# SwiGLU of a two-layer step on one core: plain 128-row tiles against Strassen's seven products over two of three token chunks

## The chip, the cores and the metric

The kernel runs on one core of a Trainium2 chip. The metric is the device time of one execution, in microseconds (us). Before the change the median of three runs is 3021.92 us, from 3016.77 to 3026.52.

## What is computed

A two-layer encoder step: layer 0 mixes tokens with forgetting attention, layer 1 with sliding-window attention, and both end with the same tail, the part that is changed:

```python
h = h + _rms(mix, norm_mix_post[i])
f = _swiglu(_rms(h, norm_ffn_pre[i]), ffn_w_gate[i], ffn_w_up[i], ffn_w_down[i])
h = h + _rms(f, norm_ffn_post[i])
gate = jax.nn.sigmoid(_rms(h, ple_norm[i]) @ ple_w_gate[i] + ple_b_gate[i])
h = h + gate * (p[i] @ ple_w_proj[i])
# _swiglu(a, g, u, d) = (silu(a @ g) * (a @ u)) @ d
# _rms(x, g) = x * rsqrt(mean(x * x) + EPS) * g
```

`mix` is the attention output times `w_out`. The model width is 1024 (`KT`=8 blocks of 128), the hidden width 2816 (`FFT`=22 blocks). The 1024 prompt tokens and 128 sample tokens make 1152 columns, in three chunks of `C`=384 (`NC3`=3). All is float32.

## The kernel before

Activations stand feature-major: a chunk is a tile of 128 partitions by 8 blocks by 384 tokens. A float32 product is made of three fast ones. Each operand is split into a rounded high part (`round_r`, L133, a cast on ACT) and the remainder (`low_part`, L139, a subtraction on DVE), and `mm3` (L229 to L231) issues weight-high times activation-high, weight-high times activation-low and weight-low times activation-high into one PSUM bank:

```python
nc.tensor.matmul(ps, w[0], a[0], start=first, stop=False)
nc.tensor.matmul(ps, w[0], a[1], start=False, stop=False)
nc.tensor.matmul(ps, w[1], a[0], start=False, stop=last)
```

A hidden tile (128 hidden features of one chunk) takes 24 such matmuls of 128x384 for gate and 24 for up (`feat`). `gu` makes both, and `act_hidden` makes Silu on ACT (L1216), times up on DVE (L1218), and the split on both. `down_tile` multiplies two hidden blocks with `w_down` into a fresh bank (6 matmuls per output block), and `down_out` adds the bank to `y` on DVE (L1252). Group g is two hidden blocks of all three chunks, so 288 gate/up matmuls and then 144 of down; a tail has 11 groups. The hidden tiles never leave SBUF.

Ahead of the groups, `serpentine` walks `w_out` over the three chunks. After a chunk's last tile come an RMS root (`plan_rms`: squares on ACT, sums on DVE L379/L381, `pstat` on PE, Newton steps on DVE L255 to L261, `prms` on PE, copy `rr` on ACT L394), the residual (`plan_residual`: a scale L469 and an add L473 for each block, the old row loaded through `st`, three buffers), a second root, and the normed and split operand (`plan_normed`, L419). After the groups comes the same with `y`, then the gate projection and, in layer 0, the projections of layer 1.

Two things order the work. `Plan` is a list scheduler that runs when the kernel is built: each step has an engine, an assumed cost, predecessors, buffers that it takes and frees, and a due time; `run` places the steps, and each engine then executes its queue in the order so found. Before, a plan covers `w_out` with group 0, and another the last group with the gates; groups 1 to 9 stand in program order, with the high-priority marks of `gu` and `down_out`. SP issues nearly all DMAs, in its own order. `act` is a pool of nine 12 KB slots (operands, `y`), `wraw`, `whi` and `wlo` hold weight units of 128x1024.

In time: projections and layer 0's attention until about 617 us, tail 0 until about 1700 (with `w_out` to about 720), layer 1's attention until about 1960, tail 1 to the end.

Of the kernel before, what the change touches and what calls it, by code (L numbers as in the profile page):

```python
# [37 lines left out]
OSP=3  # L38
SST=(1,6)
NPC=8  # L40
# [44 lines left out]
def tile_kernel(ctx: ExitStack, tc: tile.TileContext, i, o, upto=99):  # L85
# [32 lines left out]
    q2s_d = dr.tile([D, P], F32, name="q2s_d")  # L118

# [83 lines left out]
    def presplit(specs, dst):  # L203

        for u, (src, gain) in enumerate(specs):
            for q in range(4):
                cs = slice(q * 256, (q + 1) * 256)
                raw = tp.tile([P, C], F32, name="st", tag="st", bufs=STB)[:, :256]
                nc.sync.dma_start(raw, src[:, cs])
                yield  # L210
                keep = tc.keep_in_program_order
                if gain is not None:
                    nk = gain[2] // 4
                    k0 = gain[1] + q * nk
                    r3 = raw.rearrange("p (k c) -> p k c", k=nk)
                    g = gains[:, gain[0], k0:k0 + nk].unsqueeze(2).to_broadcast([P, nk, 256 // nk])
                    keep(nc.vector.tensor_tensor(r3, r3, g, MULT))
                hl = tp.tile([P, 2, C], F32R, name="sq", tag="sq", bufs=2)[:, :, :256]
                keep(nc.scalar.copy(hl[:, 0], raw))
                keep(nc.vector.tensor_tensor(hl[:, 1], raw, hl[:, 0].bitcast(F32), SUB))  # L220
                nc.sync.dma_start(dst[u][:, :, cs], hl.bitcast(F32))
                yield

# [3 lines left out]
    def mm3(ps, w, a, first, last):  # L227

        nc.tensor.matmul(ps, w[0], a[0], start=first, stop=False)  # L229
        nc.tensor.matmul(ps, w[0], a[1], start=False, stop=False)  # L230
        nc.tensor.matmul(ps, w[1], a[0], start=False, stop=last)  # L231
# [39 lines left out]
    class Plan:  # L271
# [19 lines left out]
        def run(self):  # L291
# [23 lines left out]
            while left:  # L315
# [16 lines left out]
                for u in users[n]:  # L332
                    early[u] = max(early[u], end + (LAG[engine] if engine != LOAD or steps[u][0] != LOAD else 0.0))
# [30 lines left out]
    def plan_rms(plan, src, after, out="rr", slot=None, ready=()):  # L364
# [4 lines left out]
        def square(k):  # L369
            if k:  # L370
                box[k] = t = tp.tile([P, 2, C], F32, name="sq", tag="sq", bufs=2)
# [20 lines left out]
        def copy():  # L392
            box["r"] = r = slot() if slot else tp.tile([P, C], F32, name="rr", tag=out, bufs=2)
            nc.scalar.copy(r, box["pr"][:, :C])  # L394
# [10 lines left out]

    def plan_normed(plan, src, rms, g, put, free=()):


        (r, box), out, tmp, first = rms, [], {}, []

        def scale(k):
            if not out:
                out.extend((act_slot(F32R, "ahi"), act_slot(F32R, "alo")))
                put(tuple(out))
            tmp[k] = t = tp.tile([P, C], F32, name="tmp", tag="tmp", bufs=2)
            if g is None:
                nc.vector.tensor_tensor(t, src()[:, k, :], box["r"], MULT)
            else:
                nc.vector.scalar_tensor_tensor(t, src()[:, k, :], gains[:, g, k:k + 1], box["r"], MULT, MULT)  # L419

        def high(k):
            round_r("a", out[0][:, k, :], tmp[k])

        def low(k):
            low_part(out[1][:, k, :], tmp.pop(k), out[0][:, k, :])

        done = []
        for k in range(KT):
            x = plan.add(DVE, 0.53, step(scale, k), [r] + first, takes=["tmp"] + ([] if first else ["act", "act"]))
            first = first or [x]  # L430
            x = plan.add(ACT, 0.42, step(high, k), [x])

            done.append(plan.add(DVE, 0.47, step(low, k), [x] + done[-1:],
                                 frees=["tmp"] + (["rr", *free] if k == KT - 1 else [])))
        return done
# [23 lines left out]
    def plan_residual(plan, y, rms, g, hsrc, c, then=lambda k: None):  # L459
# [16 lines left out]
        done, loads = [], []  # L476
        for k in range(KT):
            loads = [plan.add(LOAD, 0.55, step(load, k), loads, takes=["hs"])]
# [36 lines left out]
    def out_parts(ks):  # L515
# [3 lines left out]
        def split(k):  # L519
            if not parts:  # L520
                parts.extend((act_slot(F32R, "ohi"), act_slot(F32R, "olo")))
            keep(round_r("a", parts[0][:, k, :], oc[0][:, k, :]))
            keep(low_part(parts[1][:, k, :], oc[0][:, k, :], parts[0][:, k, :]))
# [548 lines left out]
    for hp in range(8):  # L1072
        pair, g = nxt, 0
        for m in ORDER:
# [8 lines left out]
            if hp == 7 and m == ORDER[0]:  # L1083
                oa0, beside = out_parts(range(KT - 1))
# [26 lines left out]
    def layer_tail(l, oc, Wo, oa0, specs_kv=(), more=None, more_rms=None):  # L1111
# [7 lines left out]
        oa, mix, a, y, b = ([None] * NC3 for _ in range(5))  # L1119
        tiles, hid = {}, {}  # L1120

        def put(where, c):
            return functools.partial(where.__setitem__, c)

        def tile_steps(key, unit, act, needs_w, needs_a, frees=(), pieces=2):
# [7 lines left out]
            for p in range(pieces):  # L1133
                x = plan.tile(3.92 / pieces, step(piece, p * n, n), [x] + needs_a[p * n:(p + 1) * n], takes=["mm"] if p == 0 else [],
# [3 lines left out]
        def serpentine(plan, W, at, act, needs, then, free):  # L1138
# [788 lines left out]
```

## Time and profile before

| quantity | value |
|---|---|
| median of three runs | 3021.92 us |
| profiled execution, its own time | 3016.32 us |
| its span in the profile | 3014.3 us |
| PE busy | 2981.8 us of the span |
| DVE, ACT, POOL busy | 1568.5, 1006.6, 197.7 us |
| DMA | 362.34 MB, mean 120 GB/s |
| granted TensorE clock | 0.999 of full speed |

PE is TensorE, PEld its weight loads, which run beside the matmuls; DVE is VectorE, ACT ScalarE, POOL GpSimd, SP the engine that issues DMAs. `L229` is line 229 of the kernel; `pgu<-ahi,whi` names the output tile and its inputs. Matmuls are pipelined, so the time that one costs in a stream is the distance between two starts, not its duration. `[2.12 <-DVE acc]` behind a row says that the engine idled 2.12 us before it, until DVE wrote `acc`.

### The profile page before, as it was taken

The numbers are of one execution on the slowest core, as the hardware profiler recorded it, in microseconds if no ns is written. First come the engines' busy times: TensorE is split into PE (matmuls) and PEld (weight loads), VectorE is DVE, ScalarE is ACT, GpSimd is POOL, SyncE is SP. The second block draws the span as 40 slices with busy tenths as digits, with TensorE's granted clock in tenths as the row PEclk, the third lists the DMA queues.
The fourth block names the chain that finished last, engine by engine and source line by source line (L and its number), as shares of the span: only waits on it lengthen the run. The fifth ranks groups of instructions, "written<-read, shape, count | busy, mean of one in ns | idle before, by whom it ended". The sixth has DMA issues, their size and how long they took to land. (4 is left out here: it accounts for less than half of the span.)

```text
span 3014.3 us, 47129 instructions
## 1 busy us (share of the span) xinstructions
PE 2981.8 (99%) x18356; PEld 2870.2 (95%) x18356; DVE 1568.5 (52%) x3657; ACT 1006.6 (33%) x2150; POOL 197.7 (7%) x324
## 2 busy tenths in 40 slices
PE   8999999999999999999999999999999999999999
PEld 8999877799999999999999998799999999999999
DVE  6253477758444444444389446658333333333486
ACT  6221367645322222221144255744311111111142
POOL 0000245400000000000000022300000000000000
PEclk9999999999999999999999999999999999999999
DMA  7364577433122222222156567434111111111064
GB/s 255 106 203 143 165 197 199 116 120 131 67 95 95 95 95 95 95 95 87 35 181 197 201 209 218 125 121 137 62 64 63 64 63 63 64 63 61 15 201 148
DMA packets 236178, 362.34 MB, mean 120 GB/s; under 512 B 32130, under 2 KB 189188, under 8 KB 235924
## 3 DMA queue, kind: packets, MB, share of 16 engines
q1 hardware_dynamic: 235956, 359.34, 37.4%
q8 instruction: 144, 2.36, 0.3%
q14 instruction: 78, 0.64, 0.1%
HBM read 263.82 MB, written 97.27 MB: 120 GB/s over the span
## 5 line engine op out<-in xcount | busy, mean ns | idle before, releaser
L229 PE MATMUL pgu<-ahi,whi 128*128 128x384 f32 x1728 | 577.4, 334 | 0.0
L230 PE MATMUL pgu<-alo,whi 128*128 128x384 f32 x1728 | 577.4, 334 | 0.0
L231 PE MATMUL pgu<-ahi,wlo 128*128 128x384 f32 x1728 | 577.3, 334 | 0.0
L229 PE MATMUL ps<-ahi,whi 128*128 128x384 f32 x1392 | 471.3, 339 | 1.0 <-ACT ev L634 0.7
L231 PE MATMUL ps<-ahi,wlo 128*128 128x384 f32 x1392 | 466.7, 335 | 1.2 <-DMA wlo<-wkq_d 1.2
L230 PE MATMUL ps<-alo,whi 128*128 128x384 f32 x1392 | 466.2, 335 | 0.0
L230 PE MATMUL pd<-hlo,whi 128*128 128x384 f32 x1056 | 357.8, 339 | 2.8 <-DVE hlo L139 2.6
L229 PE MATMUL pd<-hhi,whi 128*128 128x384 f32 x1056 | 358.0, 339 | 0.8 <-ACT hhi L133 0.8
L231 PE MATMUL pd<-hhi,wlo 128*128 128x384 f32 x1056 | 357.2, 338 | 0.0
L1252 DVE TENSOR_TENSOR y<-y,pd 128x384 f32<-128x384 f32 x480 | 262.0, 552 | 175.1 <-PE pd L231 174.7
L133 ACT CAST whi<-wraw 128x1024 fp32r<-128x1024 f32 (+3 forms) x190 | 192.9, 1024 | 472.7 <-PE pd L230 216.9
L139 DVE TENSOR_TENSOR wlo<-wraw,whi 128x1024 fp32r<-128x1024 f32 (+3 forms) x190 | 225.4, 1189 | 211.7 <-ACT whi L133 211.4
L230 PEld LDWEIGHTS pgu<-alo,whi 128*128 128x128 f32 x1728 | 324.5, 188 | 0.0
L231 PEld LDWEIGHTS pgu<-ahi,wlo 128*128 128x128 f32 x1728 | 324.5, 188 | 0.0
L229 PEld LDWEIGHTS pgu<-ahi,whi 128*128 128x128 f32 x1728 | 324.5, 188 | 0.0
L1218 DVE TENSOR_TENSOR sil<-sil,pgu 128x384 f32<-128x384 f32 x108 | 59.8, 554 | 462.1 <-PE pgu L231 462.1
L229 PEld LDWEIGHTS ps<-ahi,whi 128*128 128x128 f32 x1392 | 262.0, 188 | 7.0 <-issue 4.9
L231 PEld LDWEIGHTS ps<-ahi,wlo 128*128 128x128 f32 x1392 | 261.7, 188 | 2.2 <-DMA wlo<-wkq_d 2.2
L230 PEld LDWEIGHTS ps<-alo,whi 128*128 128x128 f32 x1392 | 262.1, 188 | 0.0
L230 PEld LDWEIGHTS pd<-hlo,whi 128*128 128x128 f32 x1056 | 198.3, 188 | 4.4 <-DVE hlo L139 4.4
L229 PEld LDWEIGHTS pd<-hhi,whi 128*128 128x128 f32 x1056 | 198.3, 188 | 1.7 <-ACT hhi L133 1.7
L231 PEld LDWEIGHTS pd<-hhi,wlo 128*128 128x128 f32 x1056 | 198.3, 188 | 0.0
(223 smaller groups left out, 4311.6 us busy)
## 6 DMA issues: line engine op xcount, KB each, us to landing
wraw<-in_w_gate SPq DMA_DIRECT2D x44, 512.0 KB
wraw<-in_w_up SPq DMA_DIRECT2D x44, 512.0 KB
wraw<-in_w_down SPq DMA_DIRECT2D x44, 512.0 KB
wpg_d<-sq SPq DMA_DIRECT2D x64, 256.0 KB
st<-h_d SPq DMA_DIRECT2D x72, 192.0 KB
wraw<-in_w_out SPq DMA_DIRECT2D x24, 512.0 KB
wkq_d<-sq SPq DMA_DIRECT2D x48, 256.0 KB
whi<-wpg_d SPq DMA_DIRECT2D x24, 512.0 KB
```

Of the source, the lines that this page charges most:

```text
L133: return nc.scalar.copy(out, in_)
L139: return nc.vector.tensor_tensor(out, x, hi.bitcast(F32), SUB)
L229: nc.tensor.matmul(ps, w[0], a[0], start=first, stop=False)
L230: nc.tensor.matmul(ps, w[0], a[1], start=False, stop=False)
L231: nc.tensor.matmul(ps, w[1], a[0], start=False, stop=last)
L1218: nc.vector.tensor_tensor(tiles[key], tiles[key], tiles.pop((key, 1))[:, :C], MULT)
L1252: nc.vector.tensor_tensor(y[c][:, f, :], y[c][:, f, :], ps[:, :C], ADD)
```

## The change

Gate, up and down are computed by the Strassen-Winograd scheme for two chunks together, cA and cB (`TAILS`: 1 and 2 in layer 0, 2 and 1 in layer 1). The third, cC = 0, stays plain.

For gate and up, a group is one weight pair (two blocks of 128 hidden features) by two halves of the model width, against two chunks by the same two halves. Instead of eight block products of 12 matmuls there are seven (`product`): operands `Y11`, `Y21`, `Y22` are halves of the normed chunks, `T1` to `T4` are sums and differences of them (`minus`, made once a tail in place, then split by `operand`), and of the weights two units are raw (A, B) and two are made of sums of halves (C, D; `s_sum`, four DVE additions of 128x512 for each matrix). The sums are held in the two `wide` buffers (tag `y`) that hold the mixed chunks cA and cB until their operands are made. Products add up in banks X, Y and Z, and X is copied out between products. The plain tiles of cC (`ps<-chi`) stand between the products, but for the first two matrices (`EARLY`), whose four plain tiles run ahead of all products.

The hidden rows then go to DRAM: 22 plain ones (`hc_d`) and 7 combinations for each of 11 pairs (`t_d`). Down is done last, as 44 ksteps for cC and 77 for the two chunks in each tail. `kstep` loads one 192 KB row back, splits it, splits half a unit of `w_down` (kept in the `act` slots as it came, changed in place between passes) and issues 12 matmuls into four banks, which are read only at the end of a pass. Each kstep takes two of the ten `row` slots (`NROW`). The additions L1252 are gone.

One `Plan` now covers a whole tail, `presplit` (the preparation of later weights) included. After down the chunks come in the order cC, cB, cA.

```diff
+NROW=10
+TAILS=((0, 1, 2), (0, 2, 1))
...
+    t_d = dr.tile([7, FFT // 2, P, C], F32, name="t_d")
+    hc_d = dr.tile([FFT, P, C], F32, name="hc_d")
...
+        operand("Y11", cA, 0)
+        operand("Y21", cA, 4)
+        operand("Y22", cB, 4)
+        minus(cA, 0, (cB, 0), (cA, 0))
+        operand("T1", cA, 0)
+        minus(cB, 0, (cB, 4), (cB, 0))
+        operand("T3", cB, 0)
+        minus(cB, 4, (cB, 4), (cA, 0))
+        operand("T2", cB, 4)
+        minus(cA, 4, (cA, 4), (cB, 4))
+        operand("T4", cA, 4)
...
+                args = {1: (s[:, 0, X1], x2()[:, X1], x2()[:, X2], ADD), 2: (s[:, 0, X2], s[:, 0, X1], x1()[:, X1], SUB),
+                        3: (s[:, 1, X1], x1()[:, X1], x2()[:, X1], SUB), 4: (s[:, 1, X2], x1()[:, X2], s[:, 0, X2], SUB)}
+                nc.vector.tensor_tensor(*args[n])
...
+                    if new:
+                        tiles[m, bank] = psmm.tile([P, 512], F32, name="p" + bank, tag="mm")
+                    a_ = acts[name]
+                    hi, lo = units_[m, u]
+                    for j in range(4):
+                        ws = slice(half * 512 + j * P, half * 512 + (j + 1) * P)
+                        mm3(tiles[m, bank][:, :C], (hi[:, ws], lo[:, ws]), (a_[:, j], a_[:, 4 + j]), new and j == 0, j == 3, more=not new)
...
+            product("X", "A", 0, "Y11", new=True)
+            copied("11", "X")
+            if not early:
+                plain(0, "A", [])
+                plain_out(0)
+            product("Z", "A", 1, "Y21", new=True, frees=[wa])
+            added("11", "Z", ["mm"])
+            product("X", "C", 1, "T2")
+            product("Y", "D", 0, "T3", new=True)
+            product("X", "C", 0, "T1", frees=[wc])
...
+            if not early:
+                plain(1, "B", [])
+                plain_out(1)
+            product("X", "D", 1, "Y22", frees=[wd])
+            product("Y", "B", 1, "T4", frees=[wb])
...
+                diff("u11", "r12", "r11")
+                store("r11", t_d[0, g], ("t", 0, g))
+                diff("r12", "r22", "r12")
+                diff("u22", "r22", "u11")
...
+        EARLY = (0, 0), (0, 1)
+        for m in EARLY:
+            matrix(*m, when=0)
         for g in range(FFT // 2):
-            for f in (2 * g, 2 * g + 1):
-                specs += [(i["w_gate"][l, f], None), (i["w_up"][l, f], None)]
...
+            def h_load():
+                hp[s] = [None, row(F32R)]
+                nc.sync.dma_start(hp[s][1].bitcast(F32), hsrc)
...
+            x = add(LOAD, 0.85, h_load, r=[hkey], after=last_row, takes=["row", "row"])
+            last_row[:] = [x]
+            x = add(ACT, 0.42, h_high, after=[x])
+            h_done = add(DVE, 0.47, h_low, after=[x])
+            x = add(ACT, 0.51, w_high, r=[wkey], after=plan.turn.get(f"w{t}", []), takes=[f"w{t}"])
+            plan.turn[f"w{t}"] = [x]
+            w_done = add(DVE, 0.6, w_low, r=[wkey], after=[x])
...
+                for d in ds:
+                    if new and start:
+                        tiles["D", d] = psmm.tile([P, 512], F32, name="pd", tag="mm")
+                    ds_ = slice(d * P, (d + 1) * P)
+                    mm3(tiles["D", d][:, :C], (parts_[s][0][:, ds_], parts_[s][1][:, ds_]), hp[s], new and start, stop, more=not new)
...
-        def gu(g, fi, c):
-            wg, wu = W.get(6 * g + 2 * fi), W.get(6 * g + 2 * fi + 1)
-            key = g, fi, c
-            for n, w in enumerate((wg, wu)):
-                tiles[key, n] = psmm.tile([P, 512], F32, name="pgu", tag="mm")
-                feat(tiles[key, n][:, :C], w, a[c])
...
-        def down_tile(g, c, f, fis=(0, 1)):
-            if 0 in fis:
-                tiles[c, f] = psmm.tile([P, 512], F32, name="pd", tag="mm")
-            fs = slice(f * P, (f + 1) * P)
-            for fi in fis:
-                wd = W.get(6 * g + 4 + fi)
-                mm3(tiles[c, f][:, :C], (wd[0][:, fs], wd[1][:, fs]), hid[g, fi, c], fi == 0, fi == 1)
...
-        def group_steps(g, order, loaded, needs, last_c, free):
...
-        for g in range(1, NG - 1):
-            for n_, t in enumerate([(0, 0), (0, 1), (0, 2), (1, 0), (1, 1), (1, 2), 0, 1, 2]):
-                if type(t) is tuple:
-                    gu(g, *t)
-                else:
-                    for f in range(KT):
-                        down_tile(g, t, f)
-                        down_out(g, t, f)
...
+                    if kind == "S2":
+                        in_place((e, 1), (e, 1), ADD, (o_, 1))
+                        in_place((e, 0), (e, 1), SUB, (e, 0))
+                    at = {"X11": (e, 0), "S2": (e, 0), "S1": (e, 1), "X22": (o_, 1), "X12": (o_, 0)}[kind]
+                    src, wkey = step(wd, *at), ("W", *at)
...
+        order2, hs_gate = (cC, cB, cA), plan.tiles[-1]
+        strassen("S3", 5, True, y_copy(cB, 4, True, True))
+        strassen("X11", 0, True, y_copy(cA, 0, False, True))
+        strassen("S2", 4, False, y_add(cA, 4, cB, False))
+        strassen("S1", 3, False, y_add(cB, 4, None, False))
+        strassen("S4", 2, False, y_copy(cB, 0, True))
+        strassen("X22", 6, True, y_add(cA, 4, None, True))
+        strassen("X12", 1, True, y_add(cA, 0, None, True))
```

The order on three queues follows. The first place is PE behind the last `w_out` tiles of tail 0. Before, a chunk's four gate and up tiles are followed by its own down tiles and by the next chunk's tiles (`ps_8522`, in pieces, as its operand `ahi_8490` comes):

```order
L231 MATMUL ps_8405<-ahi_7920,wlo_8238 128x384
L268 MATMUL prms_8470<-ident_102,ry_8452 128x128 x3
L229 MATMUL pd_8494<-hhi_8475,whi_8280 128x384
L230 MATMUL pd_8494<-hlo_8476,whi_8280 128x384
L231 MATMUL pd_8494<-hhi_8475,wlo_8281 128x384
L229 MATMUL pd_8499<-hhi_8475,whi_8280 128x384
...
L229 MATMUL ps_8522<-ahi_8490,whi_8069 128x384
L230 MATMUL ps_8522<-alo_8491,whi_8069 128x384
```

Now the four early plain tiles (the last is `ps_8391`) are followed by two roots and then by the products, of which the third needs `T2` and the weight unit C (`whi_8627`):

```order
L217 MATMUL ps_8391<-chi_7897,wlo_8236 128x384
L233 MATMUL pstat_8433<-ones_68,acc_8308 128x1 x3
L254 MATMUL prms_8463<-ident_104,ry_8444 128x128 x3
L233 MATMUL pstat_8482<-ones_68,acc_8440 128x1 x3
L254 MATMUL prms_8506<-ident_104,ry_8491 128x128 x3
L215 MATMUL pX_8521<-Y11_8476,whi_8071 128x384
...
L215 MATMUL pZ_8565<-Y21_8511,whi_8071 128x384
L216 MATMUL pZ_8565<-Y21_8511,whi_8071 128x384
L217 MATMUL pZ_8565<-Y21_8511,wlo_8072 128x384
...
L215 MATMUL pX_8521<-T2_8592,whi_8627 128x384
```

What moved: the work of one chunk alone no longer stands behind the early tiles; what stands there needs both other chunks.

The second place is DVE at the same point. Before, the splits of the next operand (`alo_8491`) are mixed with the residual of the third chunk (`mix_8117`):

```order
L1218 TENSOR_TENSOR sil_8467<-sil_8467,ps_8288 128x384
L1218 TENSOR_TENSOR sil_8403<-sil_8403,ps_8405 128x384
L473 TENSOR_TENSOR mix_8117<-mix_8117,st_8419 128x384
L139 TENSOR_TENSOR hlo_8476<-sil_8467,hhi_8475 128x384
L419 SCALAR_TENSOR_TENSOR tmp_8492<-mix_7749,gains_101,rr_8480 128x384
L139 TENSOR_TENSOR hlo_8483<-sil_8403,hhi_8482 128x384
L419 SCALAR_TENSOR_TENSOR tmp_8504<-mix_7749,gains_101,rr_8480 128x384
L139 TENSOR_TENSOR alo_8491<-tmp_8492,ahi_8490 128x384
```

Now DVE makes all seven operands, and only then, with `y_7975` and `y_7627` free again, the weight sums (`y_8622`) and unit C's low part (`wlo_8628`):

```order
L145 TENSOR_TENSOR Y21_8511<-y_7627,Y21_8511 128x384 x4
...
L1229 TENSOR_TENSOR y_7975<-y_7975,y_7627 128x384 x4
L145 TENSOR_TENSOR T2_8592<-y_7975,T2_8592 128x384 x4
L145 TENSOR_TENSOR T3_8580<-y_7975,T3_8580 128x384 x4
L145 TENSOR_TENSOR T1_8544<-y_7627,T1_8544 128x384 x4
L1229 TENSOR_TENSOR y_7627<-y_7627,y_7975 128x384 x4
L145 TENSOR_TENSOR T4_8613<-y_7627,T4_8613 128x384 x2
L1315 TENSOR_TENSOR y_8622<-wraw_8257 128x512
...
L1315 TENSOR_TENSOR y_8622<-wraw_8254,y_8622 128x512
L145 TENSOR_TENSOR T4_8613<-y_7627,T4_8613 128x384
L145 TENSOR_TENSOR wlo_8628<-y_8622,whi_8627 128x1024
```

What moved: the low part that the third product reads stands behind the operands of both chunks.

The third place is DVE between gate/up and down. Before (in a group) the last hidden tile's split is followed by the additions to `y`, eight for each chunk:

```order
L139 TENSOR_TENSOR hlo_10090<-sil_10061,hhi_10089 128x384
L1252 TENSOR_TENSOR y_8526<-y_8526,pd_10100 128x384
L1252 TENSOR_TENSOR y_8526<-y_8526,pd_10120 128x384
L1252 TENSOR_TENSOR y_8526<-y_8526,pd_10128 128x384
L217 TENSOR_TENSOR st_10034<-st_10034,gains_101 128x256
```

Now, once a tail, the last group's combinations come first, then the low parts of the first two reloaded rows (`row_13135`, `row_13137`):

```order
L1359 TENSOR_TENSOR row_13035<-row_13035,pY_13022 128x384
L1366 TENSOR_TENSOR row_12847<-row_12847,row_13035 128x384
L145 TENSOR_TENSOR wlo_13141<-wd_13012,whi_13140 128x512
L1386 TENSOR_TENSOR row_13035<-row_12847,row_13070 128x384
L145 TENSOR_TENSOR row_13135<-row_13135,row_13149 128x384
L145 TENSOR_TENSOR row_13137<-row_13137,row_13154 128x384
```

What moved: the first row of down waits in DVE's queue for the very last product (`pY_13022`) to be read and combined.

In all, PE loses 792 matmuls of 128x384 (528 of gate and up, 264 of down), DVE goes from 3659 to 4189 instructions, ACT from 1864 to 2366, and SP from 1236 to 1728 DMAs.

## Rows read from the trace of the kernel before

**Rows 1.** Page part 1: busy us, share of the span, instructions

```profile
PE 2981.8 (99%) x18356; PEld 2870.2 (95%) x18356; DVE 1568.5 (52%) x3657; ACT 1006.6 (33%) x2150; POOL 197.7 (7%) x324
```

**Rows 2.** Page part 2: granted TensorE clock in 40 slices of 75 us, tenths

```profile
PEclk9999999999999999999999999999999999999999
```

**Rows 3.** Page part 5: busy us, mean ns | idle before, releaser

```profile
L229 PE MATMUL pgu<-ahi,whi 128*128 128x384 f32 x1728 | 577.4, 334 | 0.0
...
L229 PE MATMUL pd<-hhi,whi 128*128 128x384 f32 x1056 | 358.0, 339 | 0.8 <-ACT hhi L133 0.8
...
L1252 DVE TENSOR_TENSOR y<-y,pd 128x384 f32<-128x384 f32 x480 | 262.0, 552 | 175.1 <-PE pd L231 174.7
L133 ACT CAST whi<-wraw 128x1024 fp32r<-128x1024 f32 (+3 forms) x190 | 192.9, 1024 | 472.7 <-PE pd L230 216.9
```

**Rows 4.** Timeline of PE, group 0, tail 0: start, us, engine, line, operation

```profile
800.84 0.34 PE L229 MATMUL pgu<-ahi,whi 128*128 128x384 f32 x1
...
850.76 0.34 PE L229 MATMUL pd<-hhi,whi 128*128 128x384 f32 x1
...
876.20 0.34 PE L229 MATMUL pgu<-ahi,whi 128*128 128x384 f32 x1
```

**Rows 5.** Windows: us; busy of PE, PEld, DVE, ACT, POOL; clock, DMA, GB/s

```profile
720.00:800.00 80.00, 76.11 (x430) 74.34 (x430) 49.49 (x110) 36.91 (x68) 0.00 (x0) 0.98 0.23 77
800.00:1480.00 680.00, 680.00 (x3899) 680.00 (x3898) 297.54 (x539) 140.21 (x246) 0.00 (x0) 1.00 0.27 89
2060.00:2160.00 100.00, 96.27 (x556) 94.51 (x555) 60.15 (x122) 44.44 (x78) 0.00 (x0) 1.00 0.31 102
```

**Rows 6.** Timeline of PE: the kernel's first matmuls, and the start of tail 0

```profile
7.21 0.69 PE L229 MATMUL ps<-phl,whi 128*128 128x384 f32 x1 [7.21 <-ACT phl L133]
...
11.79 0.34 PE L230 MATMUL ps<-phl,whi 128*128 128x384 f32 x1
...
723.50 0.80 PE L247 MATMUL pstat<-ones,acc 128*128 128x1 f32 x6 [2.12 <-DVE acc L381]
```

**Rows 7.** Timeline of ACT and DVE: RMS root of the third chunk, tail 0

```profile
729.46 0.48 ACT L394 COPY rr<-prms 128x384 f32<-128x384 f32 x1 [2.81 <-PE prms L268]
...
724.34 0.16 DVE L255 TENSOR_SCALAR rv<-pstat 128x3 f32<-128x3 f32 x1 [0.98 <-PE pstat L247]
...
726.59 2.01 DVE L379 TENSOR_TENSOR acc<-acc,sq 128x768 f32<-128x768 f32 x2
729.97 0.62 DVE L469 SCALAR_TENSOR_TENSOR mix<-mix,gains,rr 128x384 f32<-128x384 f32 x1 [1.37 <-ACT rr L394]
```

**Rows 8.** Timeline of DVE: back-to-back instructions of four widths, tail 0

```profile
663.70 1.22 DVE L139 TENSOR_TENSOR wlo<-wraw,whi 128x1024 fp32r<-128x1024 f32 x1
664.83 0.55 DVE L473 TENSOR_TENSOR mix<-mix,st 128x384 f32<-128x384 f32 x1
665.30 0.95 DVE L379 TENSOR_TENSOR acc<-acc,sq 128x768 f32<-128x768 f32 x1
666.17 0.55 DVE L473 TENSOR_TENSOR mix<-mix,st 128x384 f32<-128x384 f32 x1
...
701.29 0.55 DVE L473 TENSOR_TENSOR mix<-mix,st 128x384 f32<-128x384 f32 x1
701.76 0.61 DVE L469 SCALAR_TENSOR_TENSOR mix<-mix,gains,rr 128x384 f32<-128x384 f32 x1
702.29 0.55 DVE L473 TENSOR_TENSOR mix<-mix,st 128x384 f32<-128x384 f32 x1
```

**Rows 9.** SPq and DVE timelines, DVE waits: loads through three buffers

```profile
701.87 0.33 SPq L465 DMA_DIRECT2D st<-in_xT  x1
...
705.85 0.56 DVE L473 TENSOR_TENSOR mix<-mix,st 128x384 f32<-128x384 f32 x1 [0.95 <-DMA st<-in_xT]
...
DVE mix L473 <- DMA st<-in_xT: 7.7, 5, 3.0
```

**Rows 10.** Windows, columns as in rows 5: end of w_out

```profile
713.40:720.50 7.10, 7.10 (x43) 7.10 (x42) 4.75 (x5) 2.76 (x4) 0.00 (x0) 1.00 0.80 266
```

More of the change, by code (lines that the diff above doesn't have):

```diff
@@ L201, in units, with mm3 @@
         return [(ap[u], None if gain is None else (gain[0], *gain[1](u))) for u in range(ap.shape[0])]
[L203 to L222, printed above, removed]
     def parts(dram, us):
         return [(dram[u], "parts") for u in us]
[L227 to L231, printed above, removed]
+    def mm3(ps, w, a, first, last, more=False):
+        nc.tensor.matmul(ps, w[0], a[0], start=first, stop=False, skip_group_check=more)
+        nc.tensor.matmul(ps, w[0], a[1], start=False, stop=False, skip_group_check=more)
+        nc.tensor.matmul(ps, w[1], a[0], start=False, stop=last, skip_group_check=more)
     def feat(ps, unit, a, ks=range(KT)):
@@ new lines, in c_low @@
+        def c_low(k):
+            low_part(cp_[1][:, k], mix[cC][:, k], cp_[0][:, k])
+        first = []
+        for k in range(KT):
+            x = add(ACT, 0.42, step(c_high, k), r=[("m", cC, k)], w=[("chi", k)], after=first, takes=[] if k else ["act", "act"])
+            first = first or [x]
+            add(DVE, 0.47, step(c_low, k), r=[("m", cC, k), ("chi", k)], w=[("clo", k)])
+        release(["act"], [("m", cC, k) for k in range(KT)])
+        operand("Y11", cA, 0)
+        operand("Y21", cA, 4)
@@ new lines, in dpass, with yset, y_copy, evict @@
+        def dpass(steps, new, evict):
+            for n, x in enumerate(steps):
+                kstep(*x, new, n == 0, n == len(steps) - 1, evict)
+        def yset(c, first):
+            if first:
+                y[c] = act_slot(F32, "y") if c == cC else wide()
+            return y[c]
+        def y_copy(c, k0, free, create=False):
+            def evict(d):
+                eng = (ACT, DVE)[d % 2]
+                def fn():
+                    t = yset(c, create and d == 0)[:, k0 + d, :]
+                    (nc.scalar.copy if eng == ACT else nc.vector.tensor_copy)(t, tiles["D", d][:, :C])
+                x = add(eng, 0.37 if eng == ACT else 0.47, fn, r=[("D", d)], w=[("y", c, k0 + d)], after=[made.get(c)],
+                        takes=["act" if c == cC else "y"] if create and d == 0 else [], frees=["mm"] if free else [], **soon(-4.0))
+                made.setdefault(c, x)
+            return evict
@@ L1375, in layer_tail @@
+            for c in order2:
+                ra[c] = plan_rms(plan, lambda c=c: y[c], pairs(out[c]))
+                if before is not None:
+                    plan.steps[ra[c][0]][3].append(before)
+                before = ra[c][0]
+                na[c] = plan_split(plan, lambda c=c: y[c], out[c], put(a2, c), ["act" if c == cC else "y"], [ra[c][1]["read"]])
+            more(plan, tile_steps, tiles, a2, na, ra, [x for n in range(8, len(todo)) for x in split[n]])
         manual.close()
```

570 lines of the change are left out of this document (373 added, 197 removed).

## The prediction

> **What bounds the kernel now.** I read the page's busy times first: PE works 99% of the span, DVE 52%, ACT 33% [rows 1], and its granted clock stands at 9 tenths or more in every slice [rows 2]. So the time is PE's count of matmuls times their spacing, plus PE's pauses. The reader should see both apart. The spacing comes from the timeline of PE in group 0 of tail 0 [rows 4]: 288 gate/up matmuls from 800.84 to 850.76 us are 0.1733 us each, 144 of down from 850.76 to 876.20 are 0.1767. The costliest groups [rows 3] show that PE waits for nothing in them, and that DVE waits 174.7 us for PE before its additions to `y`: DVE has room in these stretches. The windows [rows 5] show where PE does pause. In the groups (800 to 1480) it is busy 680.00 of 680 us, with DVE at 297.54 and ACT at 140.21. Where each tail starts it isn't: 720 to 800 has 76.11 of 80 at a mean clock of 0.98, so 3.9 us idle and 1.6 at the lower clock, and 2060 to 2160 has 96.27 of 100, 3.7 idle. That is 9.2 us for both starts. There the RMS root and the residual of the last chunk stand between `w_out` and work for PE, and other chunks' tiles cover nearly all of it.
>
> **Saved matmuls.** 528 of gate/up at 0.1733 are 91.5 us, 264 of down at 0.1767 are 46.6: **-138.1**. All lie on the path, since PE is the path.
>
> **The start of each tail.** This is the large cost. After the last `w_out` tile PE now has four plain tiles (96 x 0.1733 = 16.6 us), the roots' small matmuls (some 2 us) and the two products on Y11 and Y21 (24 x 0.1733 = 4.2): 23 us. The third product reads unit C's low part, which stands behind the whole operand making in DVE's queue. When does it come? The third chunk's first scale needs its root's copy `rr`; that copy now stands on ACT behind the Silu of plain tile 2, and its `prms` on PE behind that tile, 48 x 0.1733 = 8.3 us after `w_out`; with the Silu, the copy and 0.51 us from copy to scale (729.46 to 729.97) [rows 7] it is 9.9 us. From that scale on to C's low part DVE has 112 instructions in its queue. Spacings [rows 8]: 384 wide with two tensors 0.47 (701.29 to 701.76), with a scalar and two tensors 0.53, 768 wide 0.87, 1024 wide 1.13; 512 wide is an estimate between 384 and 768, 0.60. A root's twelve small operations take 2.25 (724.34 to 726.59) [rows 7]. So 24 x 0.53 = 12.7, 56 x 0.47 = 26.3, 3 x 0.87 = 2.6, four weight sums 4 x 0.60 = 2.4, one 1.13, two roots 4.5: 49.6. Rows of x come through three buffers at 3.98 us from issue to use (701.87 to 705.85), and DVE waited 7.7 us for them in five waits at the start of this tail [rows 9]; I add 2. C is ready at 9.9 + 49.6 + 2 = 61.5, PE idles 61.5 - 23 = 38.5. ACT isn't the later one: its 28 casts there, at the width's share of 1.02 us [rows 3] some 0.4 each, are 11 us beside it. On waking PE pays the lower clock: at the kernel's start, after an idle stretch, the matmuls from 7.21 to 11.79 us stood 0.32 apart, the 1.2 GHz level, and 14 of them took 4.6 us instead of 2.4 [rows 6]. So 2 more, and 1 for bank X, which the first products reuse with no plain tile between. 41.5 a tail, 83 in all, less the 9.2 paid now: **+74**. Bounds a tail: 34, if the queue reorders no wait and the rows of x are there; 46, if the root comes as late as now, where PE waited 2.12 us at `pstat` [rows 6] and three rows of x wait in turn. The nearest row is the DVE spacing itself, so I keep near the middle.
>
> **From gate/up to down.** The first reloaded row's low part stands behind the last combination in DVE's queue, which needs the last product: bank read, product with gate, a weight's low part, difference, row low are 4 x 0.47 + 0.60 = 2.5 us, with the semaphore steps 3.5 a tail: **+7**. Below, 0, if PE's own end is late; above 7 a tail, if the first rows' stores and loads also come late (a load is 3.98 [rows 9]).
>
> **Down, the passes.** Each kstep adds two DVE subtractions (0.47, 0.60) and two ACT casts to PE's 12 x 0.1767 = 2.12. That is hidden by the matmuls where DVE has less than 2.12. In the first three Strassen passes it barely has: S3 adds a weight difference (1.67 a kstep), X11 none (1.07), S2 two (2.27), 55 us for 33 ksteps, and chunk cC's evictions, roots and residual, which stand among them, some 14.5. That is 70 of the 72 us which PE needs there. The queue runs ahead in the 44 plain ksteps before, so I take 3 a tail: **+6** (0 to 8 each). If this cover goes, DVE is the path and each added 512-wide operation costs its 0.60. SP's 492 added DMAs stand in one queue: a row load waits there for two `row` slots, and behind it the next rows and the halves of `w_down`; what they cost is a rival below.
>
> **Gate/up, the banks.** Bank X is copied out between products (0.47 on DVE, about as much on ACT) with one 2.1 us product of cover: **+4**, 2 a tail (0 to 7). The weight sums, 22 x 4 x 0.60 = 53 us a tail, the splits of C and D and the combinations are hidden: by count DVE has some 280 of 487 us there, as it has 297.54 of 680 now [rows 5]. The row stores wait for nothing on PE's path.
>
> **Spacing of the down matmuls.** The bank now changes every 3 matmuls in place of 6. If the 0.0034 us over gate/up is the price of a change, it doubles to 0.180; if it is the waits around a new bank, it goes to 0.1733. On 2904 matmuls that is +10 or -10; I take 0.
>
> **The tail's end.** cA's root and residual come last, beside the gates of cC and cB, 16 tiles x 4.2 us = 67 us: cost 0. Of the 480 additions that go (262.0 us of DVE [rows 3]) nothing was on the path.
>
> **Sum.** -138 + 74 + 7 + 6 + 4 = -47. The profiled execution took 3016.3 us in all, 2 over its span, so 2969; its time is 0.2% under the median of the runs, which I can't tell from noise. I say **2970**.
>
> **The rivals.** (A) The sum as it stands, chance 0.60.
>
> (B) The starts are shorter and the small terms vanish: PE at 34 us a tail gives 59 in place of 74, and without the 17 of the others 2937; half way, 2953. For it: before, DVE and ACT were ahead of PE wherever they had 44% of the time [rows 5]. Against: the 112 instructions are in one queue. Chance 0.20.
>
> (C) All at their upper bounds: 46 a tail at the start (83), 7, 8 and 7 a tail, 10 for the spacing: -138 + 83 + 44 + 10 = -1, 3015. Some of it, 2995 to 3015, has 0.12. Against: gate/up groups run at 680.00 of 680 with DVE at 44% [rows 5].
>
> (D) Slower: rows come back from DRAM too late in every kstep. Ten slots are five ksteps, so a row has 5 x 2.12 = 10.6 us from the free slot to its use. By rows it needs 0.3 to issue, 3.98 to land [rows 9], a cast and a subtraction behind one other each, about 7. At 13 us each kstep would take 2.60, 242 x 0.48 = 116 us more: 3086. It decides from 11.7 us on, where 242 x 0.21 = 51 eats the gain. For it: in the first 44 ksteps of a tail a 192 KB row and a 256 KB half unit come every 2.12 us, 216 GB/s, and at the end of `w_out` 266 GB/s already held the DMA engines at 0.80 [rows 10]. Against: that row itself, which is more than is asked for. Chance 0.08, with the variant of the next sentences in it. The Trainium skill, "DMA: Bandwidth & Descriptors", section "Anatomy of one DMA", gives a transfer a fixed part of about 2.0 us and its bytes at 436 GB/s; an estimate from that page is 2.45 us for a row, over a kstep's 2.12, and if rows came one after another the sum would be 242 x 0.33 = 80 us more, 3049. The trace does not agree that they would: 512 KB in 3.98 us would be 131 GB/s, and it shows 266 [rows 10].
>
> **How the numbers follow.** What a measurement can tell from no change is about 0.3%, 9 us around 3021.9. A and B are faster, 0.80; of C 0.06 is faster (under 3013) and 0.06 the same; D is slower. Faster 0.86, same 0.06, slower 0.08. The range takes A with its bounds, B, and C: low is -138 + 59 - 10, with nothing else, 2927, drawn in to 2932; high 3015, all upper bounds. Outside are D and the edge of B.
>
> **What would show it.** In the changed profile: PE idle once for about 38 us in each tail, before the product of `T2`, released by DVE's low part of unit C (`wlo<-y`), then some 2 us of matmuls 0.32 apart; PE busy about 138 us less; a pause of 3 to 4 us before the first `pd`; ksteps 2.1 us apart, with single waits in S2. It is wrong if PE idles under 25 us at those two places (then the queue isn't what decides), if PE waits in many products for bank copies, or if row loads (`row` from `hc_d` or `t_d`) release PE or DVE all through the passes.

## The result, and the profile after

The changed kernel takes 2987.36 us (median of four runs, 2984.95 to 2989.68) against 3023.14 before (four runs, 3016.77 to 3026.52): a ratio of 0.9884 with a 95% interval of 0.9865 to 0.9903. That is 36 us less; the forecast was 47 less, 2970. The profiled executions, by which the sum was made, took 3016.32 and 2988.70 us, so 28 less, with spans of 3014.3 and 2986.9.

The page of the profile after, its busy times and the granted clock in slices of 75 us:

```profile
PE 2873.0 (96%) x17564; PEld 2753.4 (92%) x17564; DVE 1894.1 (63%) x4187; ACT 1279.5 (43%) x2652; POOL 198.0 (7%) x324
...
PEclk9999999999799999999999999999899999999999
```

Beside [rows 1], PE has 792 matmuls less and is busy 109 us less, and its share fell from 99 to 96%: PE now pauses. That it isn't 138 less, as the forecast's sign had it, is for the larger part the lower clock, at which a matmul counts as busy for longer: by the distances between the starts, matmuls 0.25 to 0.45 us apart cost 33 us over the 0.1733 of the full clock, in place of 14. Beside [rows 2], two slices fell below 9 tenths, the eleventh and the twenty-ninth, the starts of the two tails.

Where the time went is read from the starts of PE's matmuls. A stretch runs from one such start to the next:

| stretch of PE's stream | before, us | after, us | change |
|---|---|---|---|
| start to the last `w_out` matmul of tail 0 | 715.9 | 715.4 | -0.5 |
| tail 0, to the last matmul of down | 844.9 | 825.8 | -19.1 |
| gates, layer 1's projections and attention, to tail 1 | 402.3 | 410.6 | +8.3 |
| `w_out` of tail 1 | 103.6 | 102.9 | -0.7 |
| tail 1, to the last matmul of down | 841.9 | 816.3 | -25.6 |
| gates of tail 1, to the end of the span | 105.8 | 116.0 | +10.2 |

Within the tails, where the forecast put all its terms, it is -44.7 against -47. Behind down, where it put none, some 18 us came back.

**The start.** Windows of tail 0, with the columns of [rows 5], first up to the third chunk's first residual, then up to the third product:

```profile
715.40:725.30 9.90, 9.90 (x62) 9.86 (x62) 5.83 (x18) 6.80 (x10) 0.00 (x0) 1.00 0.16 55
725.30:775.00 49.70, 19.96 (x90) 18.24 (x88) 48.02 (x112) 19.66 (x38) 0.00 (x0) 0.67 0.21 67
```

DVE is busy 48.02 of 49.70 us with 112 instructions, as many as the forecast counted (the window takes in one more at its start and leaves out the last, C's low part), while PE is busy 19.96. The timelines of PE and DVE show the end of that stretch:

```profile
774.88 0.69 PE L215 MATMUL pX<-T,whi 128*128 128x384 f32 x1 [14.33 <-ACT whi L139]
...
725.73 1.14 DVE L424 SCALAR_TENSOR_TENSOR y<-y,gains,rr 128x384 f32<-128x384 f32 x2
...
775.36 1.21 DVE L145 TENSOR_TENSOR wlo<-y,whi 128x1024 fp32r<-128x1024 f32 x1
```

The third product waits 14.33 us, at the end for unit C's high part, which needs the last weight sum. Its low part comes with DVE's next instruction, 61 us after the last `w_out` matmul at 715.4. What PE waited for up to there, in all and in how many waits:

```profile
PE pX L215 <- ACT whi L139: 14.3, 1, 14.3
PE prms L254 <- DVE ry L247: 5.6, 2, 3.0
PE pZ L216 <- DVE Y L145: 5.0, 1, 5.0
PE pstat L233 <- DVE acc L367: 4.9, 2, 4.0
```

The one long pause of the forecast is in fact four kinds of pause, since both roots and the operand Y21 stand in the same DVE queue. Tail 1 has the same with 14.3, 5.5, 5.3 and 4.6 us.

**The rest of tail 0.** PE's waits from 776 to 1300 us, and none at all from 1300 to 1541, in the passes:

```profile
PE pX L215 <- DVE row L1355: 8.8, 8, 1.8
PE pd L215 <- ACT row L139: 4.4, 2, 3.5
...
PE pX L215 <- ACT row L1353: 0.6, 1, 0.6
PE pd L216 <- DVE row L145: 0.3, 1, 0.3
```

Eight times the product of `T1` waits for DVE's copy of bank X; tail 1 has none of these. The waits of `pd` are the passage from gate/up to down. ACT's and SP's timelines, first of tail 0 and then of tail 1, show what the row's cast, which released PE, waited for:

```profile
1277.21 1.01 ACT L139 CAST row<-row 128x384 fp32r<-128x384 f32 x2 [2.36 <-DMA hc_d<-row]
...
1272.47 0.90 SPq L1529 DMA_DIRECT2D row<-hc_d  x2
1273.47 0.38 SPq L1382 DMA_DIRECT2D hc_d<-row  x1
...
2605.30 1.02 ACT L139 CAST row<-row 128x384 fp32r<-128x384 f32 x2 [2.98 <-DMA row<-hc_d]
...
2599.94 0.90 SPq L1529 DMA_DIRECT2D row<-hc_d  x2
```

The cast waits for two semaphores, one of a row's load and one of a store, and in tail 0 the view names the wrong one. By the landings in the trace the row itself, asked for at 1272.47, was there whole at 1277.14, just ahead of the cast, and the store that the view names only at 1278.18, a microsecond after the cast began. In tail 1 the view names the load, asked for at 2599.94. So PE waited for the first row to land, 4.7 and 5.3 us from its issue.

**Behind down.** Windows of PE there in tail 0 and tail 1:

```profile
1541.00:1582.00 41.00, 38.36 (x208) 38.03 (x208) 23.60 (x53) 14.17 (x23) 0.00 (x0) 0.92 0.68 233
...
2871.00:2912.00 41.00, 37.60 (x213) 37.27 (x212) 21.05 (x48) 11.22 (x17) 0.00 (x0) 0.96 0.70 237
```

Before, PE was busy all of such a stretch at a full clock:

```profile
2908.00:2950.00 42.00, 42.00 (x250) 41.92 (x250) 38.53 (x92) 18.01 (x31) 0.00 (x0) 1.00 0.73 245
```

Now the gates wait for a root, and behind the wait the clock falls. SP's, DVE's and PE's timelines show why in tail 1:

```profile
2856.27 0.32 SPq L420 DMA_DIRECT2D st<-h_d  x1
...
2872.47 0.43 SPq L175 DMA_DIRECT2D whi<-wpg_d  x1
2878.19 0.34 SPq L1666 DMA_DIRECT2D out_yT<-y  x1
...
2886.77 0.32 SPq L420 DMA_DIRECT2D st<-h_d  x1
...
2893.12 0.56 DVE L428 TENSOR_TENSOR y<-y,st 128x384 f32<-128x384 f32 x1 [2.86 <-DMA st<-h_d]
...
2898.60 0.99 PE L233 MATMUL pstat<-ones,acc 128*128 128x1 f32 x6 [3.40 <-DVE acc L367]
```

The last two rows of chunk cB's residual are asked for 30 us after the sixth. Between them SP issues the gate weights, and waits until 2878.19 for the first output row. DVE, which was ahead, idles for these rows at 2893, and PE for the root at 2898.

### The profile page after: what moved, and what is told of

Its sections match the earlier page's. It is cut to its first block, busy times and chain, and to the rows that moved or that the text cites. A ratio compares the mean times of both kernels' runs of the same rounds, so it can differ in the third digit from the quotient of the medians.

```text
span 2986.9 us, 48188 instructions
## 1 busy us (share of the span) xinstructions
PE 2873.0 (96%) x17564; PEld 2753.4 (92%) x17564; DVE 1894.1 (63%) x4187; ACT 1279.5 (43%) x2652; POOL 198.0 (7%) x324
## 5 line engine op out<-in xcount | busy, mean ns | idle before, releaser
L215 PE MATMUL ps<-ahi,whi 128*128 128x384 f32 x1008 | 343.6, 341 | 0.7 <-ACT ev L589 0.7
L217 PE MATMUL ps<-ahi,wlo 128*128 128x384 f32 x1008 | 340.1, 337 | 0.2 <-DMA wlo<-wpg_d 0.2
L215 PE MATMUL pd<-row,whi 128*128 128x384 f32 x968 | 330.5, 341 | 9.5 <-ACT row L139 9.5
L216 PE MATMUL pd<-row,whi 128*128 128x384 f32 x968 | 329.8, 341 | 0.7 <-DVE row L145 0.7
L217 PE MATMUL pd<-row,wlo 128*128 128x384 f32 x968 | 328.5, 339 | 0.0
L215 PE MATMUL ps<-chi,whi 128*128 128x384 f32 x704 | 235.5, 335 | 0.0
L217 PE MATMUL ps<-chi,wlo 128*128 128x384 f32 x704 | 235.2, 334 | 0.0
L216 PE MATMUL ps<-clo,whi 128*128 128x384 f32 x704 | 235.2, 334 | 0.0
L145 DVE TENSOR_TENSOR wlo<-wd,whi 128x512 fp32r<-128x512 f32 x198 | 135.8, 688 | 95.2 <-ACT whi L139 93.5
L215 PEld LDWEIGHTS pd<-row,whi 128*128 128x128 f32 x968 | 183.3, 189 | 11.9 <-ACT row L139 10.8
L216 PEld LDWEIGHTS pd<-row,whi 128*128 128x128 f32 x968 | 183.2, 189 | 1.8 <-DVE row L145 1.8
L217 PEld LDWEIGHTS pd<-row,wlo 128*128 128x128 f32 x968 | 183.0, 189 | 0.0
```

The lines of the kernel that those rows point to most:

```text
L145: return nc.vector.tensor_tensor(out, x, hi.bitcast(F32), SUB)
L215: nc.tensor.matmul(ps, w[0], a[0], start=first, stop=False, skip_group_check=more)
L216: nc.tensor.matmul(ps, w[0], a[1], start=False, stop=False, skip_group_check=more)
L217: nc.tensor.matmul(ps, w[1], a[0], start=False, stop=last, skip_group_check=more)
```

## The experiments

Each kernel is the changed one with the edit shown. Medians stand with their intervals against the kernel before, run on the same chip (there it took 3021.1 to 3022.4 us, and 3023.1 beside the changed kernel, so that differences between two edits are known to some 2 us); a kernel with one run has its time alone.

**Fewer tiles ahead of the products.**

```diff
-        EARLY = (0, 0), (0, 1)
+        EARLY = ((0, 0),)
```

> Edit: only the first matrix runs its two plain tiles ahead of the products; the second matrix's two go back between its products. Theory 1 (DVE's queue of operand making fixes when the third product can start, and plain tiles ahead of it fill the hole): PE's idle time at each tail's start grows from about 33 us by nearly two tiles, 7 to 8 us, and the whole by 14 to 17 us, to about 3003. Theory 2 (the hole is made by the RMS roots going back and forth between DVE and PE, which wait for PE's tiles): the roots come earlier by as much as PE has less to do, the hole stays at 33 us plus or minus 3, the time within 6 us of 2987.

3000.35 us, one run, 13 more than the change. The window from the last `w_out` matmul to the third product, in this kernel:

```profile
715.60:775.20 59.60, 21.32 (x102) 19.94 (x101) 52.80 (x126) 26.35 (x46) 0.00 (x0) 0.67 0.16 50
```

and in the changed kernel:

```profile
715.40:775.00 59.60, 29.86 (x150) 28.10 (x149) 53.85 (x129) 26.47 (x47) 0.00 (x0) 0.72 0.21 65
```

The stretch is 59.60 us in both; PE is busy 8.5 us less in it. Two tiles are two times 24 matmuls of 0.1733, 8.3 us. Theory 1: DVE sets the moment, and PE's early work only fills the time.

**More tiles ahead.** For eight later matrices unit A is split, used for the first plain tile, and freed:

```diff
+        HALF = tuple((g, up) for g in range(1, 5) for up in range(2))
-        for m in EARLY:
+        for m in EARLY + HALF:
             matrix(*m, when=0)
...
-            if not early:
+            if not done_:
                 plain(0, "A", [])
                 plain_out(0)
```

> Edit: besides the four plain tiles, the first plain tile of the next eight matrices (groups 1 to 4) also runs ahead of the products, its weight unit split for it alone and made again later. Theory 1: eight tiles are 33 us of PE work moved into each hole, and their splits and products add some 11 us to DVE's queue, so the pause falls by about 20 to 25 us a tail and the time by 40 to 50, to about 2942. Theory 2 (roots and loads of x rows make the hole): the same waits stay behind the tiles, at most 10 us a tail are won, 2967 or more.

2953.63 us, a ratio of 0.978 (0.9764 to 0.9796): 34 less than the change alone. The window up to the third product:

```profile
714.70:786.00 71.30, 60.41 (x343) 58.72 (x341) 63.31 (x138) 34.27 (x57) 0.00 (x0) 0.97 0.36 119
```

The product comes 11.7 us later, as the eight more splits on DVE take (11 us expected), and PE idles 10.9 us in place of 29.7. Theory 1 again; the gain is less than 40 to 50 because bank X's copy on ACT is now waited for seven times in tail 0 (4.7 us in all, 0.6 before), five of them in matrices that lost their tile between the first two products, and because the stretches behind down came out 3 us longer.

**The residual's loads first.**

```diff
-            plan.turn["hs"] = loads = [plan.add(LOAD, 0.55, step(load, k), loads, takes=["hs"])]
+            plan.turn["hs"] = loads = [plan.add(LOAD, 0.55, step(load, k), loads, takes=["hs"], first=first)]
...
-            res = plan_residual(plan, lambda c=c: y[c], rms, G_FPOST0 + l, h_d, c)
+            res = plan_residual(plan, lambda c=c: y[c], rms, G_FPOST0 + l, h_d, c, first=True)
```

> Edit: behind down, the loads of the old rows for the residual are placed first in SP's queue as soon as a buffer is free. Theory A (they stand in SP's queue behind weight loads and stores that wait, and land 30 us late): the DVE waits for st<-h_d behind down vanish, PE's waits for pstat there (5.2 us in tail 1, 2.8 in tail 0) and the spells at half clock behind them too, 10 to 14 us in all, to about 2975. Theory B (the DMA engines are simply full there, 0.87 busy and 296 GB/s from 2860 to 2900 us): the rows land as late, or the gate weights land later in their place; gain under 4 us.

2975.62 us, a ratio of 0.9852 (0.9837 to 0.9867), 12 less than the change. In SP's timeline the loads follow each other and stand ahead of most gate weights:

```profile
2858.10 0.32 SPq L420 DMA_DIRECT2D st<-h_d  x1
...
2860.30 2.68 SPq L420 DMA_DIRECT2D st<-h_d  x2
2863.07 0.38 SPq L175 DMA_DIRECT2D whi<-wpg_d  x1
```

PE's waits for `pstat` behind down fall from 4.8 to 1.5 us in tail 1 and from 2.6 to 1.5 in tail 0; the stretches behind down are 5.5 and 3.1 us shorter (104.9 from the last matmul of down to PE's last in place of 110.4, and 407.5 in place of 410.6). The same bytes are moved, so it is the order in SP's queue: theory A. These 8.6 us are most of the 12; the rest lies in stretches that the edit doesn't touch, where single profiles differ by 1 to 3 us.

**Eight products where there are seven.**

```diff
+            product("X", "C", 1, "T2", extra=True)
             product("X", "C", 1, "T2")
...
         strassen("S3", 5, True, y_copy(cB, 4, True, True))
+        strassen("S3", 5, True, y_copy(cB, 4, True))
```

> Edit: each gate and up matrix makes the product C times T2 twice (the sum that it goes into is then another), and the first Strassen pass of down, S3, is run twice. Eight products in each place. By the matmul count: 22 x 12 x 0.1733 = 45.8 us a tail in gate/up and 11 x 12 x 0.176 = 23.2 in down, 138 us in all, to about 3125, if PE is the path in both loops. If DVE were the path in the passes (96% by count), down would grow by DVE's share, 11 x 1.67 = 18 us a tail, or by less where DVE had been late; if bank copies are the path in gate/up, the waits for X vanish there and it grows by 4 to 5 us less in tail 0.

3111.33 us, one run. From the last `w_out` matmul to the last of down tail 1 grew by 65.2 us (69.0 by the count) and tail 0 by 60.1, where the eight waits for bank X are gone:

```profile
PE pX L215 <- ACT row L1353: 0.8, 2, 0.6
PE pX L215 <- DVE row L1355: 0.2, 1, 0.2
```

69.0 less 8.8 is 60.2. Down alone grew by 27.2 and 23.7 us for 23.2 by the count, and the stretch ahead of it by 32.9 and 41.5 for 45.8; in both tails the pause before the first down matmul is 1.0 us there, in place of 3.5 and 4.1. So, to within 4 us a tail, each saved product is worth its matmuls, and PE is the path in both loops; only bank X in tail 0 isn't covered.

**The copy of bank X on ACT.**

```diff
-            copied("21", "X", DVE if up else ACT)
+            copied("21", "X")
```

> Edit: the middle copy of bank X of an up matrix goes to ACT, as it does for a gate matrix, in place of DVE. In tail 0 PE waited eight times (8.8 us in all) for that copy on DVE, in tail 1 never. Theory 1 (the copy stands in DVE's queue behind the splits of later weights, of which tail 0 has 160 quarters and tail 1 64): with ACT the eight waits go, 8 to 10 us less in tail 0, nothing in tail 1. Theory 2 (the bank is late on any engine, since one product of cover is too short there): the waits stay, now for ACT.

2976.42 us, one run. Of PE's waits in tail 0's gate/up after the start one of 0.6 us is left; the stretch from `w_out` to down is 549.3 us in place of 562.4, in tail 1 550.5 in place of 551.2. Theory 1: the bank waited in DVE's queue. What stood just before the copy there was mostly combinations and a low part of the weight sums; the splits of later weights, which theory 1 names, are in the same queue, but whether they are what made it late was not tested apart.

**An earlier reload of the first rows.**

```diff
-        last_load, last_row, ks = [None], [wrote[FFT // 2 - 1, "u22"]], [0]
+        last_load, last_row, ks = [None], [wrote[FFT // 2 - 1, "r11"]], [0]
```

> Edit: the reload of the first rows for down may be issued when the first hidden row of the last pair is written, not only when its last combination is. Theory 1 (the pause before the first down matmul, 3.6 and 4.2 us and a spell at half clock behind it, is the late landing of the first row, 4.7 us behind its issue at 1272.5 us): the pause goes, 5 to 9 us less a tail. Theory 2, the forecast's (DVE's queue: the row's low part behind the last combination): since the low part moves ahead in the queue too, the pause goes as well, but if rows are there early and PE waits on, DVE stands as the releaser. Theory 3 (the loads of w_down before it in SP's queue and on the DMA engines make the row late wherever it stands): less than 2 us a tail.

2986.91 us, one run: nothing won. Two ksteps now stand between the last products, and the waits of `pd` are still there, 2.1 and 2.0 us, for the rows of later ksteps. ACT's waits there (1262 to 1295 us) now name the load:

```profile
ACT row L139 <- DMA row<-hc_d: 6.3, 5, 3.2
```

The DMA engines are 0.95 busy with 301 GB/s from 1265 to 1275 us in it. The pause was moved, not removed: the first row came in time, and the third, asked for at 1271.08, was cast at 1276.77. Theory 1 had the cause of the first pause, the late landing of the first row, but not the gain, which is the less than 2 us a tail of theory 3.

**The second halves of `w_down` later.**

```diff
-        for half in range(2):
+        for half in range(1):
             for f in range(FFT):
                 last_load[0] = add(LOAD, 0.75, step(wd_load, f, half), w=[("W", f, half)], after=[last_load[0], marks[-2]],
...
+                if ("W", n, 1) not in wrote:
+                    last_load[0] = add(LOAD, 0.75, step(wd_load, n, 1), w=[("W", n, 1)], after=[last_load[0], plan.tiles[-1]])
```

> Edit: the second halves of w_down are loaded one behind each kstep of the first plain pass, in place of as early as SP gets to them. Theory 3 on the seam (w_down's loads crowd the first rows on SP and on the DMA engines, which were 0.87 to 0.95 busy there in the run with the early reload): the first rows land earlier or the later ones do, and the waits of the first down matmuls for a row's cast, 4.4 us in tail 0 and 5.1 in tail 1, fall by half or more. Theory 1 (the rows can't be asked for before the last pair's rows leave their slots, whatever else is loaded): the pause before the first down matmul stays at 3 to 4 us, only what follows it changes.

2988.70 us, one run, and the same pause (5.2 us in tail 0, 4.9 in tail 1). The first halves alone keep the engines full ahead of down, as this window of the kernel shows:

```profile
1262.00:1278.00 16.00, 11.83 (x69) 11.47 (x67) 8.07 (x17) 2.80 (x6) 0.00 (x0) 1.00 1.00 350
```

So the second halves have no part in the first pause. The first row was asked for at 1271.97 and cast at 1277.44, 5.5 us later, through these full engines. That the slots held the request back, theory 1, isn't shown: what stood just ahead of it in SP's queue was a load of `w_down`, which waited for PE (0.7 us). Whether more slots, rows asked for ahead of `w_down`, or first halves loaded later would remove the pause stays open; none was tried.

**All four edits, twelve tiles ahead.** The first plain tile of the twelve matrices of groups 1 to 6, the loads first, the copy on ACT and the early reload (their diffs as above, `range(1, 7)` in `HALF`).

> Edit: all four at once, with twelve plain tiles of later matrices ahead of the products: the first tile of each matrix of groups 1 to 6, residual loads first behind down, the X copy on ACT, the early reload of rows. If the four causes are separate they add up: against 2953.6 of the run with eight tiles, 12 less from the loads, 9 from the copy, 10 to 16 from the seam and 20 to 26 from the rest of the hole (13 idle and 4 slow a tail), about 2900. If they share a wait (the DVE queue in the hole takes the four more splits as slowly as PE the tiles), 2915 to 2930.

2935.59 us, a ratio of 0.9724 (0.9702 to 0.9746): better than both kernels, but 35 short of the sum, and outside the second range too. The hole is nearly closed; PE is busy 75.00 of 79.40 us up to the third product:

```profile
716.20:795.60 79.40, 75.00 (x438) 73.63 (x436) 70.22 (x147) 39.49 (x64) 0.00 (x0) 1.00 0.44 143
```

Tail 1 is 33 us shorter than in the change, tail 0 only 13. From 800 to 1256 us PE has a new wait there; ACT's timeline at one of the longest of the twelve (3.6 us), and DVE's waits (800 to 1070 us), show what stood before the copy:

```profile
PE pX L215 <- ACT row L1353: 19.3, 12, 4.4
...
908.39 1.04 ACT L139 CAST whi<-y 128x1024 fp32r<-128x1024 f32 x1 [7.49 <-DVE y L1315]
909.35 0.47 ACT L1353 COPY row<-pX 128x384 f32<-128x384 f32 x1
...
DVE y L1315 <- DMA wraw<-in_w_up: 20.9, 7, 4.3
```

Two of the twelve, 0.6 us each, are of the kind that the changed kernel has once. In seven of the other ten the copy stands in ACT's queue right behind the cast of a weight sum, which waited 3.7 to 7.5 us for DVE's sum, and DVE waited for the weight unit to land (twelve waits, with five of 18.4 us in all for `gate`). The splits of later weights, which the next expectation names, wait in that queue too, for their stores, but further ahead; how much they delay the units was not followed. The copy comes too late once no plain tile lies between the products.

**Eight tiles in tail 0, twelve in tail 1.** Without the early reload:

```diff
-        for m in EARLY:
+        HALF = tuple((g, up) for g in range(1, (5, 7)[l]) for up in range(2))
+        for m in EARLY + HALF:
```

> Edit: as the run with all four, without the early reload of rows, and with eight plain tiles ahead in tail 0, twelve in tail 1. In that run tail 0 got a new wait, 19.3 us in twelve waits for bank X's copy on ACT, which stood behind ACT's part of the splits of later weights, that waits for a buffer to be stored. Theory 1 (a plain tile between the first two products is the cover that hides this; each matrix that gave its tile away lost it): eight in place of twelve leave about 10 to 13 us of such waits, and the hole grows by 9: no gain in tail 0, 2932 to 2940 in all. Theory 2 (only the stretch 900 to 1100 us, where the splits' stores are slow, is exposed, and eight matrices mostly end before it): at most 5 us of such waits, 2922 to 2931.

2940.51 us, a ratio of 0.9729 (0.9708 to 0.975), the upper edge of theory 1; its profiled execution, the fastest of four, took 2935.42. It is as theory 1 has it: 11.4 us in eight such waits (two of them 0.6 us each, as before), where theory 2 allowed 5, and a hole 9 us larger, which is about what the waits fell by. In tail 1, with its queues placed differently by the plan, the hole also came out 7 us larger. No version had both a closed hole and no wait for bank X in tail 0.

## Why the forecast was right, and where not

The forecast was 17 us too low by the medians (2970 against 2987.4) and 20 by the profiled runs (2969 against 2988.7), its range held, and its likeliest case was the one that came. That the tails came within 3 us of the sum is in part luck: the passes and the starts cost some 10 less than forecast, the banks and the passage to down some 8 more. By its steps:

- **Saved matmuls, -138.** Right. The extra products of the run with eight cost their matmuls to within 4 us a tail, and the spacing of the down matmuls, where forecast and bounds were 0 and 10 either way, is 0.176 us before and after, taken over those less than 0.25 us apart: a bank that changes every 3 matmuls costs no more than one every 6.
- **The start of each tail, 41.5 each.** Right, in size and in cause. C was forecast for 61.5 us after `w_out`, and its low part ended at 61; by the distances between its starts PE lost 33.4 us in tail 0 in pauses up to the first product into bank Y, 5.7 in matmuls 0.28 to 0.45 us apart, at the lower clock, and 0.7 in a return to bank X: 39.8. The parts offset each other, 33.4 for 38.5 and 5.7 for 2. The picture of one pause of 38 us was too simple: the wait before the product of `T2` is 14.3, released by C's high part, and the bound of 25 us that the prediction set for being wrong is kept only by the whole stretch, 29.7 us idle up to that product. That the queue decides rests on the runs with fewer and more tiles.
- **From gate/up to down, 3.5 each.** The size was within its bounds (4.7 and 5.4 us by the waits, and some microseconds at the lower clock behind them, as for a start), the mechanism was not. The step said that DVE's queue decides, and kept late loads for the upper bound. PE's releaser is ACT's cast of the row, which waited for the row to land, 4.7 and 5.3 us from its issue in place of 3.98, through DMA engines that are 0.99 busy from 1262 to 1278 us. DVE's last combination was done at about 1276.6, so the queue that was named came a close second.
- **The passes, 3 each.** Nothing was paid: PE waits for nothing from 1300 to 1541 us, though DVE was busy 67.60 of 70 us between 1371 and 1441, where the first three Strassen passes lie. So the count of 70 us for DVE was right (33 ksteps at 2.12 are 70 us, not the 72 that it was held against), and the queue ran far enough ahead.
- **The banks, 2 each.** Mis-sized for tail 0, 8.8 us, over its bound of 7, and 0 in tail 1. The term looked at the length of the copy, not at what stands before it in DVE's queue; the run with the copy on ACT takes the eight waits away.
- **The tail's end, 0.** This is the step that failed, and it makes up the difference: +8.3 and +10.2 us, of which the loads alone account for 3.1 and 5.5. It asked whether the gates of cC and cB cover cA's chain. They nearly do (cA's last root costs a wait of 1.4 us in tail 1); but cB's own residual was not through, because its last rows were asked for behind gate weights and a waiting store in SP's queue. In tail 1 PE's starts give 8.7 us of pauses and lower clock, 0.5 before, and some 2 us are gate matmuls that before had run ahead of the last of down. In tail 0 5.4 of the +8.3 lie ahead of layer 1's attention and 2.8 in it, with a pause of 2.4 us where it begins, of which the cause was not followed.
- **The rivals.** A came. B did not: the start was not shorter. Of C only the bank's waits came, in one tail. D did not: PE waits for no row in the passes, with rows of 192 KB every 2.1 us. The estimate of rows one after another, with the fixed part and the rate of the Trainium skill, "DMA: Bandwidth & Descriptors", section "Anatomy of one DMA", is not what the loads do here; that fit is stated for transfers by way of GpSimd, and these are issued by SP. The 131 GB/s held against it were not a reading of the trace (the 3.98 us are those of a row of 192 KB, not of 512 KB), but the 266 are.

## What to carry to other kernels

A scheme that saves work on the busy engine by tying two chunks together also takes away the work of one chunk that covered the other's preparation: count the instructions in the preparing engine's queue, and hold that against what the busy engine can still do meanwhile. Work that needs neither chunk, moved ahead, fills such a hole at the price of its own preparation, until the loop that it came from needs it as cover. Where a cost is put at nothing because something covers it, look in the queue of every engine on that chain, SP's too, for what waits in front.

## What was not expected of the hardware

Short pauses cost more than their length: behind down in tail 0 one wait of 2.6 us is followed by fifteen distances of 0.32 us, 2.2 us more than at the full clock, in a 41 us window with a mean clock of 0.92; the start of a tail has 0.72. In the run with the later second halves the DMA engines moved 350 GB/s at a busy share of 1.00 ahead of down; in the run with the early reload, 301 GB/s at 0.95.
